# A tile of the convolution and a gate ahead of the chunks' first transposes, and GpSimd's queue for the transfers of the inverse

## The chip, the cores and the metric

The kernel runs on one core of one Trainium2 chip, in one launch. The time is that of the core on the device, in microseconds (us). The kernel before took 3365.51 us in the median of three runs (3364.67 to 3365.61). The engines are TensorE (PE in the rows; PEld is its weight load), VectorE (DVE), ScalarE (ACT), GpSimd (POOL) and SyncE (SP), which here does nothing but issue transfers. A transfer is issued by the queue of one engine, in that queue's order.

## The reference

The program is two layers of one mixed block and then one block of another kind. The change touches the two layers of the first; there, for 512 tokens and a model width of 2048:

```python
for l in range(2):
    u = x @ w_in[l]
    (cb, cc, ch, cg, cq, ckv, kpe, mg, rcols, rg) = _split(u, IN_SIZES)
    y_conv = _short_conv_branch(cb, cc, ch, cg, conv_w[l])
    y_mla  = _mla_branch(cq, ckv, kpe, mg, ...)
    y_rwkv = _rwkv7_branch(rcols, rg, ...)
    x = layer_norm(alpha * x + concat([y_conv, y_mla, y_rwkv]) @ w_out[l])

# _short_conv_branch: a 3-tap causal convolution along the tokens
u = c_gate * h
y = b_gate * sum(conv_w[j] * up[:, j:j + S] for j in range(3)) * silu(gate)

# _mla_branch: q and kv come from rms-normed low-rank columns cq (512) and ckv (256),
# kpe (64) is rotated by position; the attention's output is multiplied by silu(mg)

# _rwkv7_branch: 8 heads of 64, for each token
sa    = einsum('bhvk,bhk->bhv', state, a_t)
state = state * w_t + sa * b_t + v_t * k_t
y_t   = einsum('bhvk,bhk->bhv', state, r_t)
```

The second block (attention by differences, a state-space branch, a gated merge) is not touched.

## The kernel before, in words

Activations lie with the channels on the 128 partitions and the 512 tokens along the free axis. A projection makes 128 output channels at a time: `inproj` (L187) loads the weights of 16 input tiles by two transfers of 128x8x128 (L158, on SP's queue), rounds each half to a high part (L168, ScalarE) and a low part (L169, VectorE), and `mm3` (L178) adds three matmuls for each of the 16 input tiles: 48 matmuls into one PSUM tile called acc, of which there are two.

The recurrence is done in chunks of 64 tokens. For each of four pairs of heads (j) `rwkv_prep` makes a packed tile (pk), stores it to DRAM (pack) and stores the strictly triangular 64x64 matrices of all chunks to T (L569, four transfers for each j). Phase "c" of a layer then traces these functions one after the other:

- `rwkv_inverse` (L578) inverts all 64 matrices at once by substitution. It loads T with the matrices along the partitions (L590), into a0, a1 and later a2. X0, the upper rows, takes 32 + 31 steps on VectorE; X1, the lower corner, takes 31 steps on GpSimd, while X0 goes on. A step is two instructions (L597, L598). The results go to DRAM (TI; L618 for X0, L619 for X1).
- `mla_in` makes the low-rank columns cq and ckv (`lora_in`, L762; squares by L771 on ScalarE, sums of squares by L773 on GpSimd) and kpe. The norm of the columns goes through `tok_sums` (L366), VectorE's L391, GpSimd's L396 and TensorE's L376. All are spilled to DRAM by `Spill` (L980). L855 is the matmul that follows kpe's projection.
- `rwkv_chunks` (L625) loads a packed tile (pk, L647) and its inverse (cx, L648) for each pair of heads and each of four steps along the tokens (i), transposes four parts of pk on TensorE (L663), copies the transposes out (L664), copies parts of pk into zeroed tiles (L654, L656, L668 on GpSimd; the zeroes by L634), makes a block diagonal of cx (L657, VectorE) and multiplies it (L677).

Phase "d" follows: `rwkv_out`, then `conv_branch` with four tiles of four projections, then the gates of five heads (`mla_gate`). A scheduler merges the traced functions: each engine's instructions are put in an order that follows the trace and the times by which it thinks data are ready, so the projections of phase "d" stand on TensorE between the chunks' small products. Within an engine, and within a queue, the order is then fixed: an instruction that waits holds up all behind it.

Of the kernel before, what the change touches and what calls it, by code (L numbers as in the profile page):

```python
# [18 lines left out]
P = 128  # L19
# [53 lines left out]
class K:  # L73
# [104 lines left out]
    def mm3(self, out, w, x, first=True, last=True):  # L178

        n = len(x)  # L180
        for i, ((wh, wl), (xh, xl)) in enumerate(zip(w, x, strict=True)):
            st, sp = first and i == 0, last and i == n - 1
            self.nc.tensor.matmul(out, lhsT=wh, rhs=xh, start=st, stop=False)  # L183
            self.nc.tensor.matmul(out, lhsT=wh, rhs=xl, start=False, stop=False)  # L184
            self.nc.tensor.matmul(out, lhsT=wl, rhs=xh, start=False, stop=sp)  # L185

# [235 lines left out]

def conv_branch(k: K, x, col, w, mix):
    nc = k.nc
    for j in range(4):
        c = j * P
# [75 lines left out]
def rwkv_prep(k: K, l, j, rkv, col, der, ranks, pe, T, pack, sbg):  # L502
# [63 lines left out]
    for c in range(2):  # L566
        for h in range(2):
            o = O_G + 256 * h + 128 * c
            nc.sync.dma_start(out=T[j, h, :, c].rearrange("i s t -> s i t"), in_=pk[64 * c : 64 * c + 64, :, o : o + 64])  # L569

# [7 lines left out]
def rwkv_inverse(k: K, T, TI):  # L578
# [8 lines left out]
    def load(s0, n, t0):  # L587
        t = k.b((P, PACK), tag="pk")[:, : n * (64 - t0)].rearrange("p (s t) -> p s t", t=64 - t0)
        for hs in half:
            nc.sync.dma_start(out=t[hs], in_=Tf[:, s0 : s0 + n, t0:])  # L590
        return t
# [22 lines left out]
    for q in range(31):  # L614
        step(nc.gpsimd, Xs[1], tmp1, a2[:, q], q // 2 + 1, 31 - q)
        step(nc.vector, Xs[0], tmp, a2[:, q], 16, 31 - q)
    for e, hs in enumerate(half):
        nc.sync.dma_start(out=TIf[:, e : 32 : 2], in_=Xs[0][hs])  # L618
        nc.sync.dma_start(out=TIf[:, 32 + e :: 2, 32:], in_=Xs[1][hs])  # L619


NZ = 2


def rwkv_chunks(k: K, pe, pack, TI, Y):  # L625

# [10 lines left out]
    for i in range(4):  # L637
        for jp in range(2):
# [5 lines left out]
            for u in range(2):  # L644
                j = 2 * jp + u
                pk, cx = k.b((P, PACK), tag="pk"), k.small((P, 2, 64), "cx", 3)
                nc.sync.dma_start(out=pk, in_=pack[j, i])  # L647
                nc.sync.dma_start(out=cx, in_=TI[j, :, i].rearrange("h c s t -> (c s) h t"))  # L648
                pks.append(pk)
# [12 lines left out]
                for q, o in enumerate((O_BK, O_BK + P, O_V, O_AR)):  # L662
                    nc.tensor.transpose(pt[:, q], pk[:, o : o + P], k.ident)  # L663
                nc.scalar.copy(tk[:, u], pt[:, 0:3])  # L664
# [97 lines left out]
def lora_in(k: K, x, w, c0, n, out):  # L762
# [14 lines left out]
    nc.scalar.copy(t, bcast_cols(k, rn, 1))  # L777
    out["n"] = t

# [57 lines left out]
def mla_in(k: K, x, w, scq, sckv):  # L837
# [17 lines left out]
    nc.tensor.matmul(p1, lhsT=k.dup, rhs=kr, start=True, stop=True)  # L855
    sckv["kpe"] = rope(k, p1)

# [4 lines left out]
def mla_gate(k: K, x, w, hd):  # L862
    return gate2(k, k.inproj(x, [(w[:, C_MG + hd * P : C_MG + hd * P + P], 0)]))
# [108 lines left out]
class Spill:  # L972
# [4 lines left out]

    def __setitem__(self, q, t):
        d = self.k.dp.tile([P, S], F32, name=self.k.nm(self.name))
        self.k.nc.sync.dma_start(out=d, in_=t)  # L980
        self.t[q] = d
# [18 lines left out]
def first_layer(k: K, a, l, x, xd, col, der, vec):  # L1000
# [7 lines left out]
    with k.phase(f"p{l}f", None, "right", c=6):  # L1008
# [26 lines left out]
        with k.phase(f"p{l}c", {"t": 2, "m": 2, "s": 2}, pk=4):  # L1035
            rwkv_inverse(k, T, TI)
            with k.use("c", "s"):
                mla_in(k, x, w, scq, sckv)
            Y = [k.b(tag="y") for _ in range(4)]
            rwkv_chunks(k, pe, pack, TI, Y)  # L1040
        with k.phase(f"p{l}d", {"x": 6}, e=8, e4=4):
            rwkv_out(k, Y, sbg, col, mix)
            with k.use("c"):
                conv_branch(k, x, col, w, mix)
                for hd in range(NG):
                    smg[hd] = mla_gate(k, x, w, hd)
# [845 lines left out]
```

## Time and profile before

| what | us |
|---|---|
| median of three runs | 3365.51 |
| lowest and highest | 3364.67, 3365.61 |
| the profiled execution | 3367.76 |
| its span in the profile | 3366.0 |
| TensorE busy | 3284.4 |
| VectorE busy | 1740.7 |
| ScalarE busy | 1123.9 |
| GpSimd busy | 661.4 |

Times in the rows are from the start of the span; 1.8 us of the execution lie outside it. The table's busy times are sums over the whole span; where an engine waits is seen in the timeline, where [14.00 <-DMA pk<-pack] behind a row means that the engine stood idle for 14.00 us before it and that the landing of this transfer ended the wait. In rows, out<-in are the names of the tiles. All transfers of the kernel before are issued by SP's queue (SPq); a row of it is the time that the issue took there, not the time to landing. The clock of TensorE is given as a share of its full rate of 2.4 GHz: 0.50 is 1.2 GHz.

### The profile page before, as it was taken

What the parts mean: (1) busy time and instruction counts of PE and PEld (TensorE: products, weight loads), DVE (VectorE), ACT (ScalarE), POOL (GpSimd) and SP (SyncE); (2) the same over time, 40 slices, a digit from 0 to 9 for tenths busy, and PEclk for the clock granted to TensorE, in tenths of its full rate; (3) what the DMA queues carried; (4) which work ended last, traced back from release to release, by engine and by line L of the source; (5) the groups of instructions that cost most, each with busy time, mean ns of one, the idle gap of its engine ahead of it and who ended that gap; (6) DMA issues with size and microseconds to landing.
All of it is one profiled execution on the core that took longest, in us unless ns stands there. A gap on an engine that the chain in (4) does not pass through costs nothing. (4 is left out here: it accounts for less than half of the span.)

```text
span 3366.0 us, 42736 instructions
## 1 busy us (share of the span) xinstructions
PE 3284.4 (98%) x16291; PEld 2688.8 (80%) x16291; DVE 1740.7 (52%) x2783; ACT 1123.9 (33%) x1842; POOL 661.4 (20%) x879
## 2 busy tenths in 40 slices
PE   8999899999999999999999999999999999999999
PEld 7777688877778877888777768888888888888887
DVE  4546644655864448535668865444445522322432
ACT  4332122444333322223542234343334322222332
POOL 1223322112530115221115420000000000000111
PEclk9999999999999999999999989999999999999999
DMA  6455444425554454536245544434333733333453
GB/s 172 150 177 150 123 134 123 150 76 158 178 160 127 133 172 117 149 114 186 65 153 177 175 151 136 123 117 122 121 93 115 226 102 109 100 107 103 152 146 111
DMA packets 699455, 458.98 MB, mean 136 GB/s; under 512 B 112533, under 2 KB 637098, under 8 KB 699250
## 3 DMA queue, kind: packets, MB, share of 16 engines
q1 hardware_dynamic: 699250, 456.25, 45.4%
q8 instruction: 128, 2.10, 0.3%
q14 instruction: 77, 0.63, 0.1%
HBM read 363.89 MB, written 92.27 MB: 136 GB/s over the span
## 5 line engine op out<-in xcount | busy, mean ns | idle before, releaser
L183 PE MATMUL acc<-xh,wh 128*128 128x512 f32 x3552 | 1398.1, 395 | 13.3 <-ACT c L771 5.0
L185 PE MATMUL acc<-xh,wl 128*128 128x512 f32 x3552 | 1403.4, 395 | 4.6 <-DVE wl L169 4.4
L184 PE MATMUL acc<-xl,wh 128*128 128x512 f32 x3552 | 1402.3, 395 | 2.9 <-DVE xl L176 2.8
L169 DVE TENSOR_TENSOR wl<-wr,wh 128x1024 fp32r<-128x1024 f32 (+1 forms) x508 | 665.3, 1310 | 919.1 <-ACT wh L168 907.5
L168 ACT CAST wh<-wr 128x1024 fp32r<-128x1024 f32 (+1 forms) x508 | 529.5, 1043 | 1467.7 <-PE acc L184 1192.9
L183 PEld LDWEIGHTS acc<-xh,wh 128*128 128x128 f32 x3552 | 671.3, 189 | 158.7 <-ACT c L771 6.1
L184 PEld LDWEIGHTS acc<-xl,wh 128*128 128x128 f32 x3552 | 671.3, 189 | 149.4 <-DVE xl L176 8.1
L185 PEld LDWEIGHTS acc<-xh,wl 128*128 128x128 f32 x3552 | 671.2, 189 | 146.0 <-DVE wl L169 9.0
L396 POOL TENSOR_TENSOR rr_a<-rv_a,mhalf 128x8 f32<-128x8 f32 (+1 forms) x24 | 36.9, 1538 | 516.3 <-DVE rv_a L391 516.3
L1822 POOL TENSOR_TENSOR b<-b,b 128x512 f32<-128x512 f32 x16 | 21.1, 1316 | 499.0 <-DVE b L1820 499.0
L1150 POOL TENSOR_TENSOR b<-b,b 128x512 f32<-128x512 f32 x28 | 46.9, 1677 | 158.5 <-DVE b L1133 152.3
L1820 DVE SCALAR_TENSOR_TENSOR b<-b,ps_b 128x512 f32<-128x512 f32 x32 | 22.0, 688 | 105.6 <-PE ps_b L185 105.6
L597 DVE TENSOR_TENSOR pk<-pk,pk 128x224 f32<-128x224 f32 (+59 forms) x126 | 67.5, 535 | 3.4
L598 DVE TENSOR_TENSOR pk<-pk,pk 128x224 f32<-128x224 f32 (+59 forms) x126 | 62.2, 494 | 3.5
L562 DVE TENSOR_TENSOR pk<-ps_m,mrk 128x512 f32<-128x512 f32 x32 | 22.1, 690 | 68.9 <-PE ps_m L559 68.9
L959 POOL TENSOR_TENSOR v<-v,c 128x512 f32<-128x512 f32 x16 | 20.6, 1285 | 185.6 <-ACT v L956 185.6
L818 ACT ACTIVATE a<-ps_a,nm_a,sp_a 128x128 f32<-128x128 f32 (+3 forms) x64 | 39.2, 615 | 49.5 <-DVE nm_a L815 48.1
L183 PE MATMUL acc<-n,wh 128*128 128x512 f32 x128 | 52.5, 410 | 0.0
L184 PE MATMUL acc<-n,wh 128*128 128x512 f32 x128 | 51.4, 401 | 0.0
L654 POOL COPY zm_pk<-pk 64x128 f32<-64x128 f32 x64 | 25.4, 397 | 131.2 <-DMA pk<-pack 131.1
L183 PE MATMUL ps_b<-ya,wh 128*128 128x512 f32 x128 | 50.7, 396 | 0.0
L184 PE MATMUL ps_b<-ya,wh 128*128 128x512 f32 x128 | 50.6, 396 | 0.0
(512 smaller groups left out, 3947.4 us busy)
## 6 DMA issues: line engine op xcount, KB each, us to landing
wr<-in_w_in_dram SPq DMA_DIRECT2D x336, 512.0 KB
wr<-in_w_out_dram SPq DMA_DIRECT2D x96, 512.0 KB
pack<-pk SPq DMA_DIRECT2D x32, 576.0 KB
pk<-pack SPq DMA_DIRECT2D x32, 576.0 KB
b<-xd SPq DMA_DIRECT2D x48, 256.0 KB
c<-mix SPq DMA_DIRECT2D x32, 256.0 KB
xd<-b SPq DMA_DIRECT2D x32, 256.0 KB
wr<-in_w_proj_att_dram SPq DMA_DIRECT2D x16, 512.0 KB
```

Of the source, the lines that this page charges most:

```text
L168: nc.scalar.copy(hi[:, : m * n], raw[:, : m * n])
L169: nc.vector.tensor_tensor(out=lo[:, : m * n], in0=raw[:, : m * n], in1=hi.bitcast(F32)[:, : m * n], op=ALU.subtract)
L183: self.nc.tensor.matmul(out, lhsT=wh, rhs=xh, start=st, stop=False)
L184: self.nc.tensor.matmul(out, lhsT=wh, rhs=xl, start=False, stop=False)
L185: self.nc.tensor.matmul(out, lhsT=wl, rhs=xh, start=False, stop=sp)
L396: nc.gpsimd.tensor_tensor(out=r.rearrange(flat), in0=v.rearrange(flat), in1=k.mhalf[:, 0:n], op=ALU.pow)
L562: nc.vector.tensor_tensor(out=pk[:, i, O_G:].rearrange("p (h c t) -> p h c t", h=2, c=2), in0=ps[:, :, 0:256].rearrange("p h (c t) -> p h ...
L597: eng.tensor_tensor(out=t3, in0=X[:, 0:n, c - 1 : c].to_broadcast([P, n, w]), in1=q[:, q.shape[1] - w :].unsqueeze(1).to_broadcast([P, n, ...
L598: eng.tensor_tensor(out=X[:, 0:n, c:], in0=X[:, 0:n, c:], in1=t3, op=A)
L654: nc.gpsimd.tensor_copy(out=M[kb, u, :, c * 64 : c * 64 + 64], in_=g[kb, :, c, 0])
L818: nc.scalar.activation(out=pr[:, 0:n], in_=ps[:, 0:n], func=AF.Exp, scale=scale, bias=nm, accum_out=sm)
L1150: nc.gpsimd.tensor_tensor(out=sums[0], in0=sums[0], in1=t, op=ALU.add)
```

## The change

Two things are changed in both layers. First, the convolution's tile j = 0 and the gate of head 0 are traced in phase "c", ahead of `rwkv_chunks`, and the first four transposes of each pair of heads (i = 0) are held behind the gate's last matmul (`issue_after`). Second, transfers are put on other queues. By GpSimd's go the four T stores of j = 3, all loads of the inverse, the TI stores (X1's now before X0's), the pk and cx loads of i = 0 and kpe's spill: 23 for each layer. By ScalarE's go the two spills of the norms ("n").

```diff
@@ mm3
-            self.nc.tensor.matmul(out, lhsT=wl, rhs=xh, start=False, stop=sp)
+            self.last = self.nc.tensor.matmul(out, lhsT=wl, rhs=xh, start=False, stop=sp)
@@ conv_branch
-def conv_branch(k: K, x, col, w, mix):
+def conv_branch(k: K, x, col, w, mix, js):
-    for j in range(4):
+    for j in js:
@@ rwkv_prep
-            nc.sync.dma_start(out=T[j, h, :, c].rearrange("i s t -> s i t"), in_=pk[64 * c : 64 * c + 64, :, o : o + 64])
+            queue = nc.gpsimd if j == 3 else nc.sync
+            queue.dma_start(out=T[j, h, :, c].rearrange("i s t -> s i t"), in_=pk[64 * c : 64 * c + 64, :, o : o + 64])
@@ rwkv_inverse
-            nc.sync.dma_start(out=t[hs], in_=Tf[:, s0 : s0 + n, t0:])
+            nc.gpsimd.dma_start(out=t[hs], in_=Tf[:, s0 : s0 + n, t0:])
...
     for e, hs in enumerate(half):
-        nc.sync.dma_start(out=TIf[:, e : 32 : 2], in_=Xs[0][hs])
-        nc.sync.dma_start(out=TIf[:, 32 + e :: 2, 32:], in_=Xs[1][hs])
+        nc.gpsimd.dma_start(out=TIf[:, 32 + e :: 2, 32:], in_=Xs[1][hs])
+    for e, hs in enumerate(half):
+        nc.gpsimd.dma_start(out=TIf[:, e : 32 : 2], in_=Xs[0][hs])
@@ rwkv_chunks
+NCI = 1
...
-                nc.sync.dma_start(out=pk, in_=pack[j, i])
-                nc.sync.dma_start(out=cx, in_=TI[j, :, i].rearrange("h c s t -> (c s) h t"))
+                queue = nc.sync if i else nc.gpsimd
+                queue.dma_start(out=pk, in_=pack[j, i])
+                queue.dma_start(out=cx, in_=TI[j, :, i].rearrange("h c s t -> (c s) h t"))
...
-                    nc.tensor.transpose(pt[:, q], pk[:, o : o + P], k.ident)
+                    with nullcontext() if i else k.tc.issue_after(after.ins):
+                        nc.tensor.transpose(pt[:, q], pk[:, o : o + P], k.ident)
@@ Spill
+    def put(self, q, t, queue):
         d = self.k.dp.tile([P, S], F32, name=self.k.nm(self.name))
-        self.k.nc.sync.dma_start(out=d, in_=t)
+        queue.dma_start(out=d, in_=t)
         self.t[q] = d
@@ lora_in, mla_in
-    out["n"] = t
+    out.put("n", t, nc.scalar)
-    sckv["kpe"] = rope(k, p1)
+    sckv.put("kpe", rope(k, p1), nc.gpsimd)
@@ first_layer
                 mla_in(k, x, w, scq, sckv)
+                conv_branch(k, x, col, w, mix, range(NCI))
+                smg[0] = mla_gate(k, x, w, 0)
+                after = k.last
             Y = [k.b(tag="y") for _ in range(4)]
-            rwkv_chunks(k, pe, pack, TI, Y)
+            rwkv_chunks(k, pe, pack, TI, Y, after)
...
-                conv_branch(k, x, col, w, mix)
-                for hd in range(NG):
+                conv_branch(k, x, col, w, mix, range(NCI, 4))
+                for hd in range(1, NG):
```

On TensorE in layer 0, before, the first transposes of the chunks stand in the middle of a product of the convolution (acc_3864), 106 matmuls after L855:

```order
L184 MATMUL acc_3864<-xl_165,wh_3853 128x512
L185 MATMUL acc_3864<-xh_164,wl_3854 128x512
L183 MATMUL acc_3864<-xh_175,wh_3853 128x512
L663 MATMUL ps_t_2753<-ident,pk_2744 128x128 x4
L184 MATMUL acc_3864<-xl_176,wh_3853 128x512
L185 MATMUL acc_3864<-xh_175,wl_3854 128x512
```

After, they stand behind the last matmul of gate 0 (acc_2992), 194 matmuls after L855, and the next projection (acc_3999) follows:

```order
L183 MATMUL acc_2992<-xh_307,wh_2987 128x512
L184 MATMUL acc_2992<-xl_308,wh_2987 128x512
L185 MATMUL acc_2992<-xh_307,wl_2988 128x512
L670 MATMUL ps_t_3080<-ident,pk_3071 128x128 x4
L183 MATMUL acc_3999<-xh_142,wh_3988 128x512
L184 MATMUL acc_3999<-xl_143,wh_3988 128x512
```

The transposes (L663 before, L670 after) have moved down by 88 matmuls; the next four of the same kind stay where they were, so 104 matmuls lie between the two where 191 did.

On GpSimd in layer 0, before, the zeroes of the inverse (L607), its ones (L609) and the sums of squares (L773) stand as follows; the eight memsets of L634 come just before them:

```order
L773 TENSOR_TENSOR la_2221<-la_2221,c_2351 128x512
L607 MEMSET pk_2014 128x1024
L607 MEMSET pk_2015 128x512
L773 TENSOR_TENSOR la_2221<-la_2221,c_2419 128x512
L609 MEMSET pk_2014 64x16 x2
L609 MEMSET pk_2015 64x16 x2
```

After, in the same place (L608, L610 and L780 are the same lines as L607, L609 and L773; L639 is L634), the T stores and the loads of a0 and a1 come first:

```order
L570 DMA T_344<-pk_1937 64x4x64 x4
L591 DMA pk_2011<-T_344 64x1024 x2
L591 DMA pk_2017<-T_344 64x1024 x2
L608 MEMSET pk_2014 128x1024
L608 MEMSET pk_2015 128x512
L639 MEMSET zwh_pk_3051 128x512
L639 MEMSET zw_pk_3052 128x512
L639 MEMSET zm_pk_3053 128x512
L639 MEMSET zq_pk_3054 128x512
L639 MEMSET zwh_pk_3059 128x512
L639 MEMSET zw_pk_3060 128x512
L639 MEMSET zm_pk_3061 128x512
```

The rows behind these are the other four of L639, L780, and the ones of L610, without which X0 can't begin. So the stores, the loads and the eight memsets now stand ahead of the ones on one engine.

On SP in layer 0, before, at the end of X1 (pk_2015), the TI stores and the first chunk load (L647) stand among the weight loads:

```order
L980 DMA ckv_2718<-c_2710 128x512
L158 DMA wr_3858<-in_w_in_dram 128x8x128
L158 DMA wr_3920<-in_w_in_dram 128x8x128
L619 DMA TI_345<-pk_2015 64x16x32 x2
L647 DMA pk_2744<-pack_346 128x1152
L158 DMA wr_3926<-in_w_in_dram 128x8x128
```

On GpSimd, after, at the same place of the program (L598 and L599 are the steps of X1, L653 is L647; L660, L662 and L675 are the copies L654, L656 and L668):

```order
L653 DMA pk_3071<-pack_346 128x1152
L599 TENSOR_TENSOR pk_2015<-pk_2015,t_pk_2016 128x15x2
L598 TENSOR_TENSOR t_pk_2016<-pk_2015,pk_2090 128x16
L599 TENSOR_TENSOR pk_2015<-pk_2015,t_pk_2016 128x16
L620 DMA TI_345<-pk_2015 64x16x32 x2
L660 COPY zm_pk_3053<-pk_3071 64x2x64
L662 COPY zq_pk_3054<-pk_3071 64x2x64
L660 COPY zm_pk_3053<-pk_3071 64x2x64
L662 COPY zq_pk_3054<-pk_3071 64x2x64
L675 COPY gv_pk_3067<-tk_pk_3069 64x128 x2
L653 DMA pk_3089<-pack_346 128x1152
L622 DMA TI_345<-pk_2014 64x16x64 x2
```

The chunk load of the first pair of heads has moved ahead of X1's last steps and of the TI stores; that of the second stands behind a copy of what the first transposes gave, and the X0 stores (pk_2014) behind it.

## Rows read from the trace of the kernel before

**Rows 1.** busy time, share and instructions by engine, from the page.
```profile
PE 3284.4 (98%) x16291; PEld 2688.8 (80%) x16291; DVE 1740.7 (52%) x2783; ACT 1123.9 (33%) x1842; POOL 661.4 (20%) x879
```

**Rows 2.** waits of TensorE: line, releaser, us in total, times, longest.
```profile
PE ps_t L663 <- DMA pk<-pack: 17.7, 2, 14.0
```

**Rows 3.** timeline of TensorE, layer 0: start, us, operation, [idle before <-releaser].
```profile
323.80 0.65 PE L376 MATMUL ps_s<-ident,rr_c 128*128 128x128 f32 x4 [0.47 <-POOL rr_c L396]
...
329.10 1.02 PE L855 MATMUL ps_s<-c,dup 128*128 128x512 f32 x2
...
368.19 1.11 PE L663 MATMUL ps_t<-ident,pk 128*128 128x128 f32 x4 [14.00 <-DMA pk<-pack]
...
414.74 0.60 PE L663 MATMUL ps_t<-ident,pk 128*128 128x128 f32 x4
...
424.76 1.05 PE L677 MATMUL ps_m<-rh_pk,xd_pk 128*128 128x128 f32 x8
```

**Rows 4.** timeline of TensorE, layer 1.
```profile
1291.67 1.12 PE L376 MATMUL ps_s<-ident,rr_c 128*128 128x128 f32 x4 [3.76 <-POOL rr_c L396]
...
1296.70 1.02 PE L855 MATMUL ps_s<-c,dup 128*128 128x512 f32 x2
...
1319.61 1.12 PE L663 MATMUL ps_t<-ident,pk 128*128 128x128 f32 x4 [3.71 <-DMA pk<-pack]
```

**Rows 5.** windows: stretch, us, busy by engine, then PEclk (granted clock).
```profile
368.20:373.00 4.80, 4.80 (x14) 3.93 (x15) 0.00 (x0) 0.65 (x2) 1.68 (x6) 0.51 0.48 143
1291.60:1294.60 3.00, 2.93 (x9) 2.54 (x10) 1.34 (x2) 1.07 (x2) 2.69 (x6) 0.51 0.15 51
1319.60:1325.30 5.70, 5.69 (x16) 4.63 (x17) 4.72 (x7) 0.65 (x2) 5.20 (x10) 0.50 0.11 18
```

**Rows 6.** timeline of SP's queue, layer 0: start, us, DMA issues.
```profile
277.17 1.46 SPq L569 DMA_DIRECT2D T<-pk  x2
...
279.33 1.30 SPq L569 DMA_DIRECT2D T<-pk  x2
283.75 1.13 SPq L590 DMA_DIRECT2D pk<-T  x2
...
361.75 1.31 SPq L619 DMA_DIRECT2D TI<-pk  x2
363.16 0.63 SPq L647 DMA_DIRECT2D pk<-pack  x1
...
407.43 1.29 SPq L618 DMA_DIRECT2D TI<-pk  x2
408.76 2.78 SPq L647 DMA_DIRECT2D pk<-pack  x1
...
413.36 1.40 SPq L648 DMA_DIRECT2D cx_pk<-TI  x3
```

**Rows 7.** timeline of SP's queue, layer 1.
```profile
1238.89 3.40 SPq L569 DMA_DIRECT2D T<-pk  x4
```

**Rows 8.** one line, L634: duration min/median/max ns, first and last start.
```profile
L634 POOL MEMSET zwh_pk<- x2: 517/518/518, 254.6 to 256.5; 128x512 f32 x2
```

**Rows 9.** timeline of GpSimd, layer 0.
```profile
284.46 1.28 POOL L773 TENSOR_TENSOR la<-la,c 128x512 f32<-128x512 f32 x1 [26.07 <-ACT la L771]
285.68 1.41 POOL L607 MEMSET pk<- 128x1024 f32 x2
```

**Rows 10.** timeline of all engines, layer 1, the chain before L376.
```profile
1282.60 0.15 DVE L391 TENSOR_SCALAR rv_c<-ps_s 128x4 f32<-128x4 f32 x1
...
1290.15 1.47 POOL L396 TENSOR_TENSOR rr_c<-rv_c,mhalf 128x4 f32<-128x4 f32 x1
```

**Rows 11.** windows of X0 in both layers; the third busy time is VectorE's.
```profile
293.20:407.30 114.10, 99.63 (x442) 80.74 (x442) 91.41 (x160) 24.13 (x32) 46.09 (x72) 0.94 0.40 107
1250.80:1360.60 109.80, 102.33 (x446) 82.97 (x445) 91.83 (x158) 24.43 (x32) 48.85 (x73) 0.95 0.43 115
```

**Rows 12.** timeline of VectorE, layer 0, the block product.
```profile
417.24 1.09 DVE L657 TENSOR_TENSOR xd_pk<-cx_pk,blk 128x256 f32<-128x256 f32 x3 [2.22 <-DMA cx_pk<-TI]
```

More of the change, by code (lines that the diff above doesn't have):

```diff
@@ L617, in rwkv_inverse, with rwkv_chunks @@
     for e, hs in enumerate(half):
-        nc.sync.dma_start(out=TIf[:, e : 32 : 2], in_=Xs[0][hs])
-        nc.sync.dma_start(out=TIf[:, 32 + e :: 2, 32:], in_=Xs[1][hs])
+        nc.gpsimd.dma_start(out=TIf[:, 32 + e :: 2, 32:], in_=Xs[1][hs])
+    for e, hs in enumerate(half):
+        nc.gpsimd.dma_start(out=TIf[:, e : 32 : 2], in_=Xs[0][hs])
 NZ = 2
-def rwkv_chunks(k: K, pe, pack, TI, Y):
+NCI = 1
+def rwkv_chunks(k: K, pe, pack, TI, Y, after):
     nc = k.nc
@@ L978, in __setitem__ @@
     def __setitem__(self, q, t):
+        self.put(q, t, self.k.nc.sync)
+    def put(self, q, t, queue):
         d = self.k.dp.tile([P, S], F32, name=self.k.nm(self.name))
-        self.k.nc.sync.dma_start(out=d, in_=t)
+        queue.dma_start(out=d, in_=t)
         self.t[q] = d
```

## The prediction

> **What bounds the kernel now.** I read the busy line first: TensorE works 3284.4 us of the 3366.0, so time goes only where TensorE stands idle or runs at a low clock [rows 1]. The waits of TensorE come next. The largest is for the load of a packed chunk tile (pk<-pack), 17.7 us in two waits [rows 2]. The timeline puts them in place. In layer 0 the first four transposes of the chunks (L663, called T1 here) start at 368.19 after 14.00 us idle, and the L376 before them, which needs the rank column that GpSimd makes at L396, after 0.47 [rows 3]. In layer 1 it is 3.71 us at T1 and 3.76 at L376 [rows 4]. Behind these waits the clock stands at half, 1.2 GHz: granted 0.51 for 4.8 us behind the first, 0.51 for 3.0 and 0.50 for 5.7 in layer 1 [rows 5]. Work of x us at half clock would take x/2 at full, so they cost 2.4, 1.5 and 2.85 us.
>
> SP's queue shows why T1 waits. The load that it needs was issued at 363.16, right behind the X1 stores (TI<-pk, 361.75), which wait for GpSimd's last step of X1; it landed 5.0 us later, when T1 starts [rows 6]. So T1 came too early for its data.
>
> **What goes.** L0: 14.00 + 2.4 + 0.47 = 16.9 us. L1: 3.71 + 2.85 + 3.76 + 1.5 = 11.8 us. Together 28.7, the most that this change can give. No instruction of TensorE is added.
>
> **The moved transposes.** By the order, 106 convolution matmuls stand between L855 and T1 in layer 0, and 194 afterwards (192 in layer 1 for 80). In the timeline a matmul comes every 0.227 us at full clock: L855 at 329.10, T1 due at 354.19, 106 matmuls and L855's own two passes (1.02 us) between [rows 3]. So T1 moves to 328.6 + 1.0 + 194 x 0.227 = 373.6, where 328.6 is L855 without the 0.47. Its load lands by 361.75 + 5.0 + what GpSimd's queue adds, some 6 us (below): 373. T1 meets data about as it comes due. The next four (T2) then have 104 matmuls before them for 191, so T2 is due at 373.6 + 23.6 + 0.9 = 398.1, where 0.9 is the transposes and small products between. In the trace T2 was at 414.74 [rows 3]. So the data of T2, behind the end of X0 (VectorE's half of the inverse), are what comes late next. X0 ended at 407.3 in the old run [rows 11].
>
> **The new queue.** GpSimd issues 23 transfers a layer. The trace of before holds none of GpSimd's, so the price c of one issue is bounded by neighbours. Low: SP's shortest, 0.47 (three cx loads in 1.40); its T and TI stores take 0.65 to 0.73 [rows 6]. High: SP's longest, 2.78 for a pk load [rows 6]. Between lie GpSimd's own instructions over a whole tile, 0.52 (memset) to 1.28 (L773) [rows 8, 9]. I take c = 1.3, the dearer of GpSimd's own rows: it works on an issue itself, over as many partitions as on a tile. The ends stay for the range.
>
> What is behind these issues is the start of X0. In the old run: T stores at 277.17 to 280.63, loads at 283.75 (3.1 us to landing), X0 from 293.2 [rows 6, 11]. Afterwards one in-order engine does: four stores (from 276.8, when VectorE is done with the last product), 3.1 us landing, four loads, two memsets 1.41, eight zero memsets that ran in idle time before, at 254.6 (8 x 0.47, since four lie between the two zwh_pk starts, 254.6 and 256.5), one L773 1.28, then the ones (about 0.3). X0 can start at 276.8 + 4c + 3.1 + 4c + 6.8 = 286.7 + 8c, and not before 293.2. With c = 1.3: 297.1, 4 us late [rows 8, 9]. Layer 1, from the T stores at 1238.9 less the store of pack before them (0.4) [rows 7]: 1248.4 + 8c = 1258.8, 8 late against 1250.8 [rows 11]. All that is issued behind on GpSimd, the sums of L773 and L396, waits with it.
>
> **Who waits for X0.** (a) L376, through VectorE's L391, which by the order stands behind 37 instructions of X0 in layer 0 (39 before) and 41 (44) in layer 1. Layer 0: X0 late by 4 us moves L376's data to about 323.2, and TensorE comes at 322.2 (five rows earlier in the order): 1.0 us. Layer 1: L396 ran at 1290.15 because X1 steps stood before it; now it stands before X1, so the old 3.76 would go. But L391 comes 7 us later than at 1282.6 (that is 31.8 after X0's start, less a us for fewer of them): 1289.6, plus L396 1.5: L376 at 1291.2, TensorE there at 1288.6: 2.6 us, and the half clock of 1.5 stays [rows 4, 5, 10]. (b) T2. X0 needs 91.4 us of VectorE in a window of 114.1 [rows 11]; the idle 22.7 is mostly TensorE's own stall and weights that came late behind SP's blocked queue, so I give X0 96 us: end at 393.1 in layer 0, then c + 5.0 to the second pk load: 399.4 against 398.1, 1.3 us late. Layer 1: end 1354.8, data 1361; T1 at 1340, T2 1364.5: none. (c) The inverse's way back. In the old run X0's end to the block product L657 took 9.9 us [rows 11, 12]: 4.6 from the end of the TI issue (408.72) to the cx loads, 3.9 from there to L657 [rows 6]. Now it is X0's end + pk issue c + two TI stores 2c + 4.6 landing + cx issue c + 3.5 = 8.1 + 4c, so 406.4. L677, the first reader, followed T2 by 10.0 us (414.74 to 424.76) [rows 3], so is due at 409.4: covered by 3.0. If c = 2.3 the cover is gone at 410.9, but by then T2 itself is later.
>
> Sum at c = 1.3: L0 16.9 - 1.0 - 1.3 = 14.6. L1 11.8 - 2.6 - 1.5 = 7.7. Together 22.3, so the profiled execution's 3367.76 becomes 3345.5. That execution lay 2.25 above the median of the runs, 3365.51, so I predict 3343.3 and round to 3344, the cost of new waits being one-sided.
>
> SP loses 25 issues, and its weight loads no longer stand behind the TI stores: nothing is lost there. ACT takes the two spills of the norm columns, an issue each, where TensorE waits for nothing of it. X1 on GpSimd: begins with a2, which is loaded behind VectorE's step 32, so up to 4 us later with 2c; its end moves by some 6 us, which is the 6 used for T1.
>
> The Trainium skill has a rule against this change. "SBUF — State Buffer", on the trap that it calls "DVE blocks DMA", says that a transfer issued from GpSimd has its descriptors written by GpSimd's cores, and that these are shut out while VectorE runs a two-port operation; it gives about 0.62 us alone and 3.1 beside a copy. X0's steps are tensor-tensor products, which the rule as given there does not name, and the trace of before has no such transfer to test it on. By its 3.1 as an estimate of c the sum would be a loss of about 7 us. Its case is the third rival, priced from rows.
>
> **The rivals.** The deciding number is c; from c = 1.3 to 2.27 the sum falls. At 2.27 (SP's 2.78 is above it) X0 starts at 304.9 and 1266.6. L0: L376 waits 8 + 1.6 of clock, T2 0.7: gain 6.6. L1: L376 waits 10.6 + 1.5: 11.8 - 12.1 = -0.3. Sum 6.3. That is 16.5 us of gain for 1 us of c.
> 1. Everything is covered: c up to 0.9, X0 no later than 293.9. The full 28.7: 3367.76 - 28.7 - 2.25 = 3336.8. For it: SP's issues take 0.47 to 0.73. Against: GpSimd's own rows over a tile, 1.28.
> 2. The front wait eats it: c of 2.2 to 3.1, or the pieced stores (T, TI) half as dear again as the others, as on SP (0.65 to 0.47), and plain ones above 1.9. Then L376 replaces T1 as the long wait, and the gain is 0 to 6.7: 3359 to 3372, around 3363, no change that can be told.
> 3. Slower: GpSimd's in-order queue is dearer than 3.1 an issue, as where it stands still beside VectorE's X0 (80% busy in that window). Then the T chain alone starts X0 18 us late, L376 waits 15 in layer 0 and 17 in layer 1, with 1.5 of clock each, and T2 another 1: 28.7 - 36 = 7 lost at c = 3.1, so 3372.5, and 16.5 more for each us above. It decides from c = 2.65 on for the sign, from 3.1 for what can be measured.
>
> If the T stores cost 2.6 and the loads 1.3, the mean of the eight is 1.95: gain 11.6, 3354, inside the forecast's case.
>
> **How the numbers follow.** Under 0.2% (6.7 us) this kernel's runs can't be told from no change. Forecast case (c 0.9 to 2.2, 3338 to 3358) 0.55, full cover 0.24, front wait 0.14, slower 0.07. Of the forecast case all is faster by over 0.2%, of the full cover too; 0.02 of the front wait goes with them. So faster 0.81, same 0.12, slower 0.07. The range takes in the full cover (3336) and reaches into rival 2, to 3361; about 0.17 lie outside.
>
> **What would show it.** The new trace should hold: no idle above 2 us before the first transposes in either layer; GpSimd's transfers about 1.3 us apart where they stand in a row, and X0 starting at about 297 and 1259; the wait at L376 about 1 us in layer 0 and 2 to 3 in layer 1; T2 within 2 us of its 398; no wait at L677. It is wrong where GpSimd issues at 0.7 or under (rival 1), or where the longest wait sits at L376 (rival 2), or where a new wait stands at L677, T1 or among the convolutions that I have not named.

## The result

| kernel | median us | runs | ratio to the kernel before, 95% interval |
|---|---|---|---|
| before | 3365.56 | 3364.67 to 3370.6 | |
| changed | 3343.64 | 3340.96 to 3346.24 | 0.9933 (0.992 to 0.9945) |

The change makes the kernel faster by 21.9 us in the medians, 0.67% by the ratio. The forecast was 3344 in a range of 3336 to 3361. The profiled executions, 3367.76 before and 3341.93 after, lie 25.8 apart; that of before stood 2.2 above its median and that of after 1.7 below, so 4 of the 25.8 are the spread of single runs.

The page of the changed kernel shows three queues of the kernel's own transfers where there was one: q1 is SP's, q0 (software_dynamic) GpSimd's, q10 ScalarE's. The columns are packets, MB and share.

```profile
PE 3280.2 (98%) x16291; PEld 2687.1 (80%) x16291; DVE 1747.2 (52%) x2783; ACT 1124.5 (34%) x1842; POOL 704.7 (21%) x925
...
q1 hardware_dynamic: 675666, 444.19, 44.4%
q0 software_dynamic: 3296, 11.01, 1.2%
...
q10 hardware_dynamic: 576, 1.05, 0.1%
```

TensorE is busy 4.2 us less than before [rows 1], though it has as many instructions: its mean granted clock is 0.991 where it was 0.988. The span is 25.8 us shorter.

The timeline of TensorE in layer 0 of the changed kernel; L670 are the transposes, L862 is L855 of before, and L855 here is the first matmul of kpe's projection.

```profile
252.57 0.50 PE L183 MATMUL acc<-xh,wh 128*128 128x512 f32 x1 [1.88 <-ACT c L778]
...
304.35 0.60 PE L376 MATMUL ps_s<-ident,rr_c 128*128 128x128 f32 x4
306.89 0.62 PE L855 MATMUL acc<-xh,wh 128*128 128x512 f32 x1 [1.94 <-ACT la L778]
...
321.83 0.60 PE L376 MATMUL ps_s<-ident,rr_c 128*128 128x128 f32 x4
...
327.74 1.02 PE L862 MATMUL ps_s<-c,dup 128*128 128x512 f32 x2
...
372.62 0.60 PE L670 MATMUL ps_t<-ident,pk 128*128 128x128 f32 x4
...
397.18 0.60 PE L670 MATMUL ps_t<-ident,pk 128*128 128x128 f32 x4
```

The 14.00 us before the first transposes [rows 3] are gone: they start at 372.62 with no idle time, and the second ones at 397.18. L376 waits no longer. What is new is the 1.94 us at 306.89, before kpe's projection: it needs an acc buffer that ScalarE's L778 clears, and ScalarE did that behind other copies. The load of the first transposes landed at 369.44, 3.2 us before they began. Layer 1:

```profile
1271.27 0.60 PE L376 MATMUL ps_s<-ident,rr_c 128*128 128x128 f32 x4
...
1274.01 1.02 PE L862 MATMUL ps_s<-c,dup 128*128 128x512 f32 x2
...
1318.43 0.60 PE L670 MATMUL ps_t<-ident,pk 128*128 128x128 f32 x4
...
1343.45 0.66 PE L670 MATMUL ps_t<-ident,pk 128*128 128x128 f32 x4 [0.30 <-DMA pk<-pack]
```

Both waits of 3.7 us [rows 4] are gone, and 0.30 is left before the second transposes. Adding up the idle times over 0.25 us in the stretches of the chunks (240 to 620 and 1190 to 1600) gives 29.06 us before and 9.37 after.

GpSimd, layer 0. The first columns are start and time on its queue.

```profile
274.76 2.71 POOL L570 DMA_DIRECT2D T<-pk  x4 [20.80 <-DVE pk L562]
281.66 2.09 POOL L591 DMA_DIRECT2D pk<-T  x4 [4.19 <-DMA T<-pk]
...
288.86 1.31 POOL L780 TENSOR_TENSOR la<-la,c 128x512 f32<-128x512 f32 x1
290.09 0.66 POOL L610 MEMSET pk<- 64x16 f32 x4
290.83 2.95 POOL L780 TENSOR_TENSOR la<-la,c 128x512 f32<-128x512 f32 x2
...
310.15 2.25 POOL L591 DMA_DIRECT2D pk<-T  x2 [0.71 <-DVE pk L598]
```

Four T stores take 2.71 us, 0.68 each; the loads 0.52 each; the two of a2, in shorter pieces, 1.1 each. The T stores landed 4.2 us behind the issue, against SP's 3.1 [rows 6]. The ones (L610) are set at 290.09. VectorE in the same place, and at the start of X0 in layer 1:

```profile
288.19 3.08 DVE L169 TENSOR_TENSOR wl<-wr,wh 128x1024 fp32r<-128x1024 f32 x1 [6.46 <-ACT wh L168]
291.19 1.31 DVE L598 TENSOR_TENSOR pk<-pk,pk 128x63 f32<-128x63 f32 x1
...
1239.19 1.31 DVE L598 TENSOR_TENSOR pk<-pk,pk 128x63 f32<-128x63 f32 x1
```

X0 starts at 291.2 where it was 293.2 [rows 11], and TensorE's work ahead of it stands 2.3 us earlier than before: X0 is 0.3 us late in layer 0. In layer 1 it starts at 1239.2 where it was 1250.8, with all ahead 17.4 earlier: 5.8 us late. About 2 of these are VectorE's order: the ones were set by 1236.8, but an L169 that waited for ScalarE until 1237.70 stands before X0.

SP in layer 0, from 344 to 369, now holds nothing but weight loads; the kernel before had SP waiting in this stretch for kpe's spill and for X1's end:

```profile
344.54 24.31 SPq L158 DMA_DIRECT2D wr<-in_w_in_dram  x5
```

### The profile page after: what moved, and what is told of

The parts are those of the page before. It is cut to its first block, busy times and chain, and to the rows that moved or that the text cites. A ratio compares the mean times of both kernels' runs of the same rounds, so it can differ in the third digit from the quotient of the medians.

```text
span 3340.2 us, 42777 instructions
## 1 busy us (share of the span) xinstructions
PE 3280.2 (98%) x16291; PEld 2687.1 (80%) x16291; DVE 1747.2 (52%) x2783; ACT 1124.5 (34%) x1842; POOL 704.7 (21%) x925
## 5 line engine op out<-in xcount | busy, mean ns | idle before, releaser
L169 DVE TENSOR_TENSOR wl<-wr,wh 128x1024 fp32r<-128x1024 f32 (+1 forms) x508 | 667.1, 1313 | 885.7 <-ACT wh L168 878.1
L396 POOL TENSOR_TENSOR rr_a<-rv_a,mhalf 128x8 f32<-128x8 f32 (+1 forms) x24 | 36.9, 1538 | 516.0 <-DVE rv_a L391 516.0
L598 DVE TENSOR_TENSOR pk<-pk,pk 128x224 f32<-128x224 f32 (+59 forms) x126 | 70.0, 556 | 3.4
L599 DVE TENSOR_TENSOR pk<-pk,pk 128x224 f32<-128x224 f32 (+59 forms) x126 | 65.0, 516 | 3.5
L1853 POOL TENSOR_TENSOR b<-b,ln 128x512 f32<-128x512 f32 x16 | 20.7, 1292 | 151.5 <-DVE b L1852 126.0
```

What stands on the lines that cost most here:

```text
L169: nc.vector.tensor_tensor(out=lo[:, : m * n], in0=raw[:, : m * n], in1=hi.bitcast(F32)[:, : m * n], op=ALU.subtract)
L396: nc.gpsimd.tensor_tensor(out=r.rearrange(flat), in0=v.rearrange(flat), in1=k.mhalf[:, 0:n], op=ALU.pow)
L598: eng.tensor_tensor(out=t3, in0=X[:, 0:n, c - 1 : c].to_broadcast([P, n, w]), in1=q[:, q.shape[1] - w :].unsqueeze(1).to_broadcast([P, n, ...
L599: eng.tensor_tensor(out=X[:, 0:n, c:], in0=X[:, 0:n, c:], in1=t3, op=A)
```

## The experiments

Each was timed beside the kernel before on the same chip. That kernel took 3365.08, 3363.95 and 3367.80 us (medians) on the three chips of the experiments, so runs on different chips are compared by their ratios to it. Other differences to the changed kernel go by its 3342.5 to 3343.6.

**The changed kernel again** (no edit).

> The changed kernel itself once more, to see what of its trace repeats. Theory A (the removed waits are exact, the clock's dips behind short idles are not): the idle times of TensorE come back to 0.1 us, the 1.94 us before L855 of layer 0 among them, but the dips to half clock behind them differ in place, so that two executions differ by some us; median 3341 to 3347. Rival B (the dips at 1751 and the longer ones near 955 and 1905 belong to the change): they stand at the same places again with the same lengths, and the execution takes 3341.9 within 1.

3342.54 (3340.46 to 3343.8), ratio 0.993 (0.9917 to 0.9942). Idle times came back to 0.1 us, the 1.94 at L855 too; only the 0.30 before layer 1's second transposes is absent. The clock did not come back. Here are the first idle of layer 0 in this run and the clock of the 3.4 us behind it:

```profile
253.71 0.68 PE L183 MATMUL acc<-xh,wh 128*128 128x512 f32 x1 [1.88 <-ACT c L778]
```

```profile
253.66:257.09 3.43, 3.38 (x8) 2.72 (x9) 2.80 (x5) 0.00 (x0) 1.43 (x1) 0.53 0.78 215
```

and the clock in the same place of the changed kernel's first profile, behind the same 1.88 us (its row at 252.57 above):

```profile
252.57:256.00 3.43, 3.42 (x15) 2.85 (x16) 2.80 (x5) 0.00 (x0) 1.39 (x1) 1.00 0.73 217
```

PEclk is the number before the last two: 0.53 and 1.00. Eight matmuls were done in 3.4 us in the one, fifteen in the other. Later stretches differ too: from 1740 to 1760 the granted clock is 0.91 in the first profile and 1.00 here, from 950 to 985 0.76 and 0.80. Theory A holds in these two executions: the waits belong to the kernel, the short dips to the execution. The longer dips near 955 and 1905 stand in both.

**The order alone.** All transfers on SP, as before:

```diff
-            queue = nc.gpsimd if j == 3 else nc.sync
+            queue = nc.sync          # T stores; so too the inverse's loads, TI, pk, cx, kpe and n
```

> The reordering alone: a tile of the convolution and a gate ahead of the first transposes, every transfer on SP's queue as before. Theory A (the order was what mattered): the 14.00 and 3.71 us before the first transposes go, since their load lands at about 366 and they now come at about 374; the 3.76 at L376 of layer 1 may stay, as GpSimd's L396 may again stand behind X1's steps; 3341 to 3352. Rival B (the queues were what mattered: SP issues the chunk loads only behind blocked weight loads): 5 us or more stay before the first or second transposes in each layer, 3352 to 3362.

3356.43 (3351.01 to 3360.65), ratio 0.9972 (0.9961 to 0.9984): 8.6 us faster than before, 13 short of the changed kernel. The 14.00 and 3.71 are gone, and 3.17 stays at L376 of layer 1, as A had it; but the time is in B's range, because other waits came. TensorE in layer 0:

```profile
368.97 0.50 PE L183 MATMUL acc<-xh,wh 128*128 128x512 f32 x1 [2.56 <-ACT wh L168]
...
402.38 0.66 PE L668 MATMUL ps_t<-ident,pk 128*128 128x128 f32 x4 [1.60 <-DMA pk<-pack]
```

The first is a projection that waits for its weights, the second the second transposes. ScalarE's cast of these weights had waited 12.31 us for their load:

```profile
367.88 1.04 ACT L168 CAST wh<-wr 128x1024 fp32r<-128x1024 f32 x1 [12.31 <-DMA wr<-in_w_in_dram]
```

and SP, which issues them, stood still from 350.05 to 359.21, because the TI stores (L620) wait there for X1's end:

```profile
348.93 1.12 SPq L158 DMA_DIRECT2D wr<-in_w_in_dram  x2
359.21 1.31 SPq L620 DMA_DIRECT2D TI<-pk  x2
...
361.39 14.38 SPq L158 DMA_DIRECT2D wr<-in_w_in_dram  x4
```

**The queues alone.** No gate or convolution ahead of the chunks, no hold:

```diff
-                conv_branch(k, x, col, w, mix, range(NCI))
-                smg[0] = mla_gate(k, x, w, 0)
-                after = k.last
```

> The queues alone: the transfers by GpSimd's and ScalarE's queues as in the changed kernel, convolution and gates traced after the chunks as before, no hold on the transposes. Theory A: the first transposes stand about 113 matmuls behind L855, so they come due at about 355 in layer 0 while their load lands at about 370: 12 to 15 us of idle time stay there, and 3 to 6 in layer 1; 3355 to 3366. Rival B (queues mattered): less than 5 us in all before the transposes, 3341 to 3350.

3374.51 (3368.84 to 3375.48), ratio 1.0022 (1.0013 to 1.0031): slower than before. Theory A for layer 0; in layer 1 the wait is not 3 to 6 but 14.92:

```profile
369.31 1.11 PE L669 MATMUL ps_t<-ident,pk 128*128 128x128 f32 x4 [13.81 <-DMA pk<-pack]
...
1330.01 1.11 PE L669 MATMUL ps_t<-ident,pk 128*128 128x128 f32 x4 [14.92 <-DMA pk<-pack]
```

In layer 1 the kernel before issued that load from SP at 1314.4, while X1 still ran; now it is in GpSimd's order behind X1's steps:

```profile
1326.12 0.60 POOL L653 DMA_DIRECT2D pk<-pack  x1 [0.24 <-issue]
```

The parts do not add: 8.6 us faster and 9.4 slower alone, 21.9 faster together.

**X0 later.** Each of the four T stores issued three times, the extra ones to DRAM that nobody reads:

```diff
+            for n in range(2 if j == 3 else 0):
+                nc.gpsimd.dma_start(out=k.dp.tile([4, 64, 64], ...), in_=pk[64 * c : 64 * c + 64, :, o : o + 64])
```

> The changed kernel with each of GpSimd's four T stores of j = 3 issued three times, the extra two into DRAM that nobody reads: eight more issues of about 0.67 us before the inverse's loads, so X0 starts about 5.4 us later in both layers, as if an issue cost c = 1.2 to 1.3, the prediction's value. Theory A (the prediction's chain is right and only c was over-priced): waits of 1 to 5 us come at L376 or before the second transposes in each layer (the second have 0.3 us of idle now in layer 1 and about 1.7 of slack in layer 0), with half clock behind some: 8 to 14 us more than the changed kernel, 3351 to 3358. Rival B (there is slack behind X0 that the prediction did not see): under 4 us more, 3343 to 3348.

3362.96 (3359.48 to 3364.88), ratio 0.999 (0.9982 to 0.9999): 19 to 20 us more than the changed kernel, twice what A had. X0 (L600) starts here, in layer 0 behind two L165 that each wait for ScalarE's cast; GpSimd had set the ones (L612) before:

```profile
292.83 0.63 POOL L612 MEMSET pk<- 64x16 f32 x4
...
294.12 1.27 DVE L165 TENSOR_TENSOR wh<-wr,wh 128x512 fp32r<-128x512 f32 x1 [3.78 <-ACT wh L164]
299.56 0.69 DVE L165 TENSOR_TENSOR wh<-wr,wh 128x512 fp32r<-128x512 f32 x1 [4.17 <-ACT wh L164]
300.18 0.22 DVE L600 TENSOR_TENSOR pk<-pk,pk 128x63 f32<-128x63 f32 x1
...
1253.36 0.22 DVE L600 TENSOR_TENSOR pk<-pk,pk 128x63 f32<-128x63 f32 x1
```

which, with all ahead of it 0.7 us earlier in layer 0 and 7.9 later in layer 1, is 9.7 and 6.3 us later than in the changed kernel, not 5.4. GpSimd accounts for a part only: in layer 0 the ones are set 3.4 us later by the same reckoning, at 293.5, and the other 6 us are VectorE's, whose order the scheduler made anew (in the changed kernel both L165 stand behind X0's first steps). In layer 1 the ones are 5.1 us later. TensorE waits at L376 (L857 is kpe's projection) and then before the first transposes, whose load stands behind the X1 that began late:

```profile
307.63 0.65 PE L376 MATMUL ps_s<-ident,rr_c 128*128 128x128 f32 x4 [2.30 <-POOL rr_c L396]
...
378.96 0.66 PE L672 MATMUL ps_t<-ident,pk 128*128 128x128 f32 x4 [2.04 <-DMA pk<-pack]
...
1265.46 0.65 PE L376 MATMUL ps_s<-ident,rr_c 128*128 128x128 f32 x4 [1.50 <-POOL rr_c L396]
1267.77 0.51 PE L857 MATMUL acc<-xh,wh 128*128 128x512 f32 x1 [1.67 <-ACT la L780]
...
1338.16 1.11 PE L672 MATMUL ps_t<-ident,pk 128*128 128x128 f32 x4 [4.53 <-DMA pk<-pack]
```

By the start of the same instructions, layer 0's stretch lost 7.1 us for 9.7 of lateness and layer 1's 13.7 for 6.3. So waits at L376 and at the first transposes come back when X0 and X1 are late, but the two layers give no common price for one us, and the order is another.

**X0 later still.** The same with six extra stores for each.

> As the run with X0 about 5.4 us late, but with each T store of j = 3 issued seven times: 24 more issues of about 0.67 us, so X0 starts some 16 us later in both layers, as if an issue cost 2.6. Theory A (the chain from X0 to TensorE holds in full once the slack is spent): every us of lateness behind the first few is idle time of TensorE in each layer, at L376, the first or the second transposes: 24 to 36 us more than the changed kernel, 3367 to 3380, so not faster than the kernel before. Rival B (the waits lie beside each other and the scheduler moves other work into them): 3355 to 3366.

3364.4 (3361.12 to 3368.07), ratio 1.0 (0.9991 to 1.0009). X0 started 12.0 and 13.0 us late by the same reckoning (302.61 and 1261.61), not 16: the extra issues took 0.62 us each and ran while GpSimd would otherwise have waited for the stores to land (4.19 us in the changed kernel), so that the ones came 10 us later in layer 0 (300.08). About 22 us more than the changed kernel, by the ratios some 3 more than the run before: rival B in size, though it does not tell how much is the order that the scheduler chose anew.

**The late half of the queues alone.** T stores and the inverse's loads back on SP.

```diff
-            queue = nc.gpsimd if j == 3 else nc.sync
+            queue = nc.sync
...
-            nc.gpsimd.dma_start(out=t[hs], in_=Tf[:, s0 : s0 + n, t0:])
+            nc.sync.dma_start(out=t[hs], in_=Tf[:, s0 : s0 + n, t0:])
```

> The changed kernel with the T stores of j = 3 and the inverse's loads back on SP; GpSimd keeps the TI stores, the chunk loads of i = 0 and kpe's spill, ScalarE the norms' spills. The order on TensorE is the kernel's before up to L376. Theory A (the early half only makes X0 late and shifts the order; the late half is what frees SP's weight loads): no wait before L855 in layer 0, the late weights (2.56 us in the order-only run) and the waits of the second transposes (1.60 and 1.83) gone, but L376 of layer 1 waits 3.2 again because L396 stands behind eighteen X1 steps: 3343 to 3350. Rival B (the early half is what pays): as order alone, 3352 to 3358.

3346.94 (3341.08 to 3347.64), ratio 0.9942 (0.993 to 0.9955), which can't be told from the changed kernel's 0.9933: what the early half (T stores and the inverse's loads by GpSimd) adds is not seen in the time. No wait for weights, none before kpe's projection; 0.82 us stand before the first transposes of layer 0, and at L376 of layer 1 there is the old wait, as A had it:

```profile
1272.93 0.96 PE L376 MATMUL ps_s<-ident,rr_c 128*128 128x128 f32 x4 [3.10 <-POOL rr_c L396]
```

**The early half alone.** T stores of j = 3 and the inverse's loads by GpSimd, the rest on SP.

```diff
-        nc.gpsimd.dma_start(out=TIf[:, 32 + e :: 2, 32:], in_=Xs[1][hs])
+        nc.sync.dma_start(out=TIf[:, 32 + e :: 2, 32:], in_=Xs[1][hs])
...          # so too X0's, pk and cx of i = 0, kpe and n
```

> The other half: T stores of j = 3 and the inverse's loads by GpSimd, all else on SP as before, convolution and gate ahead of the chunks. Theory A: the 1.94 us before L855 in layer 0 stays, L376 of layer 1 has no wait, but SP's TI stores and chunk loads hold weight loads and the second transposes, so 3 to 8 us of idle time behind the first transposes come back: 3347 to 3356. Rival B: as the changed kernel, 3341 to 3346.

3365.1 (3358.16 to 3370.72), ratio 1.0001 (0.9992 to 1.001): nothing is left of the gain, worse than A's 3347 to 3356. The waits are those that A named, but larger, at 5.94 in layer 0 and 5.50 in layer 1:

```profile
376.86 0.79 PE L183 MATMUL acc<-xh,wh 128*128 128x512 f32 x1 [5.94 <-ACT wh L168]
```

With the early half X1 ends later: SP issues nothing from 350.84 until X1's stores go at 368.17, 17.3 us, where with the order alone it was 9.2.

**X1's stores alone back on SP.** The changed kernel with two transfers moved:

```diff
-        nc.gpsimd.dma_start(out=TIf[:, 32 + e :: 2, 32:], in_=Xs[1][hs])
+        nc.sync.dma_start(out=TIf[:, 32 + e :: 2, 32:], in_=Xs[1][hs])
```

> The changed kernel with one thing undone: the two TI stores of X1 are issued by SP again, where they wait for X1's end with weight loads behind them. Theory A (what GpSimd's queue gains is that SP's weight loads no longer stand behind a waiting store): SP issues nothing for some 10 to 20 us before X1's end, ScalarE's cast waits as long for its weights, and TensorE stands idle 2 to 6 us for them at the projections behind the first transposes in each layer, with half clock behind: 5 to 14 us more than the changed kernel, 3348 to 3357. Rival B (the issue time alone is saved, two issues of 0.65 us): within 2 us of the changed kernel, 3341 to 3346.

3357.78 (3351.47 to 3362.51), ratio 0.9968 (0.9957 to 0.9979), against 0.9933: about 12 us lost by two transfers that take 1.42 us to issue. SP:

```profile
344.31 7.90 SPq L158 DMA_DIRECT2D wr<-in_w_in_dram  x2
367.50 1.42 SPq L620 DMA_DIRECT2D TI<-pk  x2
369.02 7.20 SPq L158 DMA_DIRECT2D wr<-in_w_in_dram  x3
```

From 352.21 to 367.50 it issues nothing. ScalarE's cast waits for the weights behind:

```profile
373.52 1.04 ACT L168 CAST wh<-wr 128x1024 fp32r<-128x1024 f32 x1 [16.55 <-DMA wr<-in_w_in_dram]
```

and TensorE at last, in layer 0 and in layer 1:

```profile
376.48 0.50 PE L183 MATMUL acc<-xh,wh 128*128 128x512 f32 x1 [3.61 <-DVE c L409]
...
1329.41 0.80 PE L183 MATMUL acc<-xh,wh 128*128 128x512 f32 x1 [5.84 <-DVE c L409]
```

The named releaser, VectorE's L409, had just ended: it reads an acc buffer that TensorE needs, and it stands on VectorE behind the L169 of the same late weights, which had waited 7.52 us for this cast (7.43 in layer 1). So the late weights reach TensorE through VectorE's order. Theory A is shown: the store itself is short, what waits behind it is the cost.

**The late half with X1 held.** As the late half; X1 and what follows it in the inverse are traced behind `mla_in`, and X1's sixth step is put behind L396:

```diff
     a2 = load(32, 32, 32)
+    yield            # from here on traced behind mla_in
...
+        with k.tc.issue_after(k.rr.ins) if q == 5 else nullcontext():    # k.rr is L396 of ckv
             step(nc.gpsimd, Xs[1], tmp1, a2[:, q], q // 2 + 1, 31 - q)
```

> The late half alone (as the run before the last), with one thing more: GpSimd's X1 is held behind L396 from its sixth step on, so L396 of ckv stands behind ten X1 instructions instead of eighteen in layer 1; layer 0 as it was. Theory A: the 3.2 us at L376 and the half clock behind it go, nothing else comes back, since X1 ends no later than it does in the changed kernel: 3 to 5 us less than the late half alone, 3338 to 3344, the fastest of all. Rival B: X1's end moves by as much as L396 gains and the first transposes of layer 1 wait for it: no gain over the late half.

3340.3 (3337.88 to 3342.25), ratio 0.9925 (0.9911 to 0.9938). The wait at L376 in layer 1 is gone, and 1.40 us stand before the first transposes in layer 0:

```profile
374.22 0.66 PE L672 MATMUL ps_t<-ident,pk 128*128 128x128 f32 x4 [1.40 <-DMA pk<-pack]
...
1273.77 0.60 PE L376 MATMUL ps_s<-ident,rr_c 128*128 128x128 f32 x4
```

**The same again**, beside the next run.

> The late half with X1 held once more, on the same chip as the two runs beside it, as the measure for the fifth buffer: 3338 to 3343, idle times of TensorE as in its first run within 0.1 us, dips of the clock at other places.

3340.27 (3338.57 to 3342.56), ratio 0.992 (0.9906 to 0.9933). The idle times came back to 0.1 us (1.31 for the 1.40); the two dips to half clock behind layer 0's waits of 1.88 and 1.89 us (0.50 from 252.71 and 283.43 in the first run) did not.

**With a fifth buffer.**

```diff
-        with k.phase(f"p{l}c", {"t": 2, "m": 2, "s": 2}, pk=4):
+        with k.phase(f"p{l}c", {"t": 2, "m": 2, "s": 2}, pk=5):
```

> The late half with X1 held, and a fifth buffer for pk, so that the loads of the first and second chunk tiles need not wait for a buffer of the inverse. Theory A: the 1.40 us before the second transposes of layer 0 go (their load then lands before X0's end), all else as it was: 0 to 3 us less than with four buffers, 3337 to 3341. Rival B (GpSimd's queue holds the loads behind X1's steps anyway): the wait stays, 3338 to 3343.

3338.3 (3334.77 to 3340.55), ratio 0.991 (0.9895 to 0.9925). The expectation misnamed the place: the 1.40 stood before the first transposes. It is gone, and L376's 0.47 too; the stretches of the chunks hold 7.13 us of idle time, against 8.9 and 9.0 with four buffers.

This version has the lowest median. The interval of its ratio overlaps that of four buffers (0.9906 to 0.9933) widely and that of the changed kernel (0.992 to 0.9945) by a little, so that it is faster than the changed kernel is likely, not shown.

## Why the prediction was right, and where it was not

**The total** came out (3344 against 3343.6), its parts did not, and that the sum fits so closely is luck. It took 28.7 us off and added 6.4 for new waits. In truth nearly all of the 28.7 was gained, none of the named new waits came, and smaller things that it had not named took their place. By the prediction's own signs, no wait at the first transposes, the second at their time and none at the block product came true; the price of an issue, the start of X0 and the waits at L376 did not.

**What bounds the kernel, and what goes**: right. The waits of 14.00, 0.47, 3.71 and 3.76 are gone, and the half clock behind them. Going by the start of the same instructions in both timelines, the changed kernel gained 16.7 us over layer 0's stretch for the 16.9 worked out, and 11.3 over layer 1's for 11.8. In layer 0 this hides two things of nearly the same size: the new wait before kpe's projection cost 3.6, and the kernel before had two stretches of half clock behind waits of 1.88 and 1.89 us that this execution of the changed kernel does not have, worth 3.4. In the kernel before:

```profile
253.47:256.89 3.42, 3.42 (x9) 2.64 (x9) 2.68 (x5) 0.00 (x0) 3.42 (x6) 0.50 0.81 228
284.19:287.61 3.42, 3.42 (x10) 2.64 (x9) 0.00 (x0) 0.19 (x1) 3.15 (x4) 0.50 0.75 175
```

The second execution of the changed kernel has both again (0.50 from 253.87 and from 284.58), so these 3.4 us are not the change's.

**Where the transposes go**: right. The first came at 372.6 for 373.6, the second at 397.2 for 398.1, no wait in layer 0.

**The price of an issue**: wrong, c = 1.3 against 0.52 to 0.7 where several stand in a row (1.1 for the a2 loads). The value was taken from an instruction of GpSimd over a tile; SP's own rows, 0.47 to 0.73 [rows 6], were the near ones. So rival 1, full cover, was the true case by its condition, and its 3336.8 would have been right had nothing else come. The longest issue of GpSimd took 1.15 us, beside X0's steps on VectorE, so nothing near the 3.1 of the third rival came.

**The start of X0**: the formula gives, with 0.6, 291.5 in the old run's time, so 293.2 at the earliest; measured 0.3 late. In layer 1 it gives 1253.2, 2.4 late, and 5.8 were measured: the stores took 3.9 us to land for 3.1, and X0 then stood some 2 us behind VectorE's L169. The formula has no term for VectorE's order. In the kernel before too X0 began right behind an L169 (at 292.09, after 8.05 us for ScalarE), 4.3 us after the ones. Two smaller slips: the 91.4 us of VectorE count all its work in that window, and X0 took 99.9 and 99.6 for the 96 given, though the load of the second transposes still landed at 395.53, 1.7 us before they came in layer 0; and the 410.9 in (c) is 410.4 by its own terms, on which nothing hangs.

**What X0's lateness costs**: not settled, but probably under-priced. The prediction put 6.4 us on X0 being 4 and 8 us late. The run with X0 9.7 and 6.3 us late lost 19 to 20. In kind the step was right (L376 first), but the first transposes, which the prediction had about covered, waited most there, because X1 and its load go with X0. Much of that run's lateness came from VectorE's new order, so what c = 1.3 would have cost in the changed kernel's own order no run shows.

**SP's queue**: here a step failed. "Nothing is lost there" gave the move of the TI stores no value. The order-only run shows what they cost on SP once the transposes no longer hide it: 2.56 us for late weights and 1.60 for the second transposes' load in layer 0. The runs with stores back on SP show 3.61 to 5.94. Before the change SP stood as long (352.58 to 361.75) and TensorE had no wait for weights, only the one at the transposes, which covered it; with the transposes moved, weights are late next. The prediction asked only which data of the transposes would be late next, and not which weights. Rivals and forecast missed that each half of the change needs the other.

The Trainium skill has a rule that would have misled here as well: "DMA: Bandwidth & Descriptors", section "Issuing engines are not separate DMA queues", says that issuing from several engines saves only the time of the issue on the sequencer, usually small beside the transfer. By it the two X1 stores are worth their 1.42 us of issue; the run that put them back lost about 12. The measurement decides: SP's issue that waited for X1 held the weight loads behind it for 15.3 us.

**What was not named**: the 1.94 us before kpe's projection, with 3.4 us of half clock behind, some 3.6 us in all. It came with the early half, which moved TensorE's L366 20 rows down, so that the projection follows L376 at once while ScalarE is still at its copies. It is absent from the runs without the early half, and those of them that have the late half are as fast within the intervals. The other 3 us between 3336.8 and 3343.6 I put down to the clock, which differs between executions of the same kernel as shown above, and to the spread of the runs. In the profiles 28.0 of the 28.7 are gained over the two stretches and 25.8 in the whole span; the medians lie 21.9 apart. This part is argued: no run tells the two apart.

**The rivals.** Front wait (2) and slower (3): not in the changed kernel. That lateness behind GpSimd can eat the whole gain is seen in the run with X0 up to 10 us late, which is within 0.1% of the kernel before. That the cost grows by 16.5 us for each us of c is not borne out: the run with 24 extra stores lost some 3 us beyond the one with eight, by the ratios.

What stays open: how much of the two runs with late X0 is X0 and how much the scheduler's new order, since more issues on GpSimd also moved L376 up on TensorE (by 18 rows in layer 1) and X0 behind two casts on VectorE.

## What to carry to other kernels

When a transfer has to wait for data, look at what stands behind it on its queue; a short store in the wrong queue costs what its followers wait, which may show only when a longer wait beside it is gone. When a wait is taken away, ask for each input of the stretch, weights too, how far behind it is. A change in two parts should be tried in parts: here one part gained 8.6 us, the other lost 9.4, and both gained 22.

## What the runs showed of the hardware

- An issue by GpSimd took 0.52 us (a0, a1) to 0.68 (T stores), 0.9 for X1's TI stores and 1.1 for the a2 loads, the last two in pieces of 128 bytes; the T stores landed about 4 us behind the issue, SP's 3.1.
- The same idle time of 1.88 us was followed by 3.4 us of half clock in one execution and by none in another of the same kernel.
- VectorE's product that starts at 288.19 took 3.08 us, where it takes 1.23 otherwise, and X0's first step 1.31 for 0.22, while GpSimd ran sums of squares (288.86, 290.83). The Trainium skill, "SBUF — State Buffer", section "Who interferes with whom", says that a VectorE operation with two SBUF inputs and a GpSimd one that reads SBUF contend for one port; the rows agree.
